# First norm of a decoder layer: scale and bias applied behind the transposes, with features on partitions

## The chip, the cores and the metric

The kernel runs on one core of a Trainium2 chip. The metric is the device time of one execution in microseconds (us). Five engines run their own instruction queues in order and meet through semaphores: TensorE (PE, matmuls; its weight loads are the rows PEld), VectorE (DVE), ScalarE (ACT), GpSimd (POOL) and SyncE (SP, which issues DMAs here). SBUF is the on-chip memory with 128 partitions, PSUM the memory that TensorE writes; one PSUM bank holds 128x512 floats.

## What is computed

A decoder layer over 512 tokens of 1024 features, all in float32. Only its beginning matters here:

```python
h = layer_norm(x, ln0_g, ln0_b)                  # (x - mu) * rsqrt(var + eps) * g + b
proj = h @ w_in[l]
q, f_logit, i_val, g_out, v_pool, gate_a, gate_b = jnp.split(proj, IN_SPLITS, axis=-1)
y_a = hgrn2_mixer(q, f_logit, i_val, g_out, ...) @ w_hg_branch[l]    # 8 recurrent heads
...
h = layer_norm(ALPHA * h + mix @ w_out[l], ln1_g[l], ln1_b[l])
...
```

So `h` has two readers: the projections, which want it with features on partitions, and the residual sum before the second norm, which wants it with tokens on partitions. What follows (mixers, expert retrieval over 16384 experts, a third norm) is the same in both programs.

## The kernel before

Tokens are worked on in four blocks of 128 (`NB`), features in eight chunks of 128 (`NCK`). The stage in question makes `h` and the first half of the values, `h @ w_in[:, 2048:2560]`:

- `load_x` and `load_w` issue DMAs on SP: each block of x as two halves of 256 KB, and four tiles of the value weights (`raw`, 512 KB each), two tiles to one buffer.
- `stats0` (VectorE, L277 and L279) takes mean and variance of a block, `deviation0` (ScalarE, L283) the square root, `affine0` (VectorE, L290, L293, L294) the norm: for each half of 512 features, (x - mean) * gain, and that times the reciprocal deviation plus bias. Gain and bias are the same for all tokens, so they are needed in every partition: four row loads of 2 KB (L299) and four matmuls of a row of ones with such a row (L312) put them into four PSUM banks `gb0`. The normalized block is `hres`, the residual.
- `transpose_split` turns a block by eight TensorE transposes (L162) into two PSUM banks `fp`, ScalarE copies each bank to the rounded part `xthi` (L167), VectorE subtracts to get the remainder `xtlo` (L168). A product of float32 matrices is three matmuls of such parts (`mm3`, L154 to L156).
- `split` makes the same two parts of a weight tile: a cast on ScalarE (`wh`, L149), a subtraction on GpSimd (`wl`, L150).
- `first_v(blk)` projects a block: 24 matmuls of 128x512 into a bank, which `put_v` copies out. Chunks 0 and 1 need the first weight tile, 2 and 3 the second, and so on.

The order of VectorE, ScalarE, SP and TensorE in this stage is that of the code (`manual_schedule`): for each block `affine0`, the next block's `stats0`, the transposes, the next block's `deviation0`, the weight tiles that `W0` names (the second and third behind block 0, the fourth behind block 1), and the projection of the block before. Eight matmuls on ones (`WARM`) stand ahead. GpSimd, and work that is coded outside that region, is placed by the scheduler that builds the program: small constants (`cmask`, `dtab`, `scT`, `pos` on GpSimd; `smask`, `reset`, `rc` on VectorE) are coded behind the stage and stand inside it in the queues.

Behind the stage `tok_half` does the second half of the values (L154 to L156 again), then the heads run: 36 tiles of the other projections in `slots`, with the attention parts `att0` to `att4` between them. `gain_bias(n)` loads gain and bias of a norm into all partitions, two DMAs of 512 KB.

## Time and profile before

| what | us |
|---|---|
| median of 3 runs | 1769.32 |
| lowest and highest run | 1764.86, 1771.26 |
| the profiled execution | 1768.82 |
| its span (first to last instruction) | 1767.1 |
| TensorE busy in the span | 1741.1 (99%) |
| VectorE busy in the span | 1317.2 (75%) |
| ScalarE, GpSimd busy | 799.1, 420.0 |

The profile is of one execution. The rows further down are read like this: start and length in us (a length with xN spans N instructions), engine, line of the kernel, operation, output <- inputs, shapes. What stands in brackets is the idle time of the engine just before and what ended it. A row's start plus its length is its end. The time of the profiled execution is 1.7 us more than its span.

### The profile page before, as it was taken

Reading aid. Unit: us, or ns where it says so; the run is one execution under the profiler, and the core shown is the slowest. Engines: PE = TensorE matmul, PEld = TensorE weight load, DVE = VectorE, ACT = ScalarE, POOL = GpSimd, SP = SyncE. Lnnn points to the kernel's source line nnn. Section 1 sums busy time; section 2 is a strip of 40 time slices with the busy share of each in tenths; the row PEclk is TensorE's granted clock in tenths of the full one; section 3 lists DMA queues with packets and bytes.
Section 4 is the critical chain, followed back from the end, with each engine's and each line's share of the span. In section 5 each row is a group of like instructions: output and inputs, shape, how many; then the busy total and the mean of one; then the engine's idle time right before and its main releaser. Section 6 shows DMA issues by size and latency. Waiting matters only on the chain.

```text
span 1767.1 us, 24739 instructions
## 1 busy us (share of the span) xinstructions
PE 1741.1 (99%) x9697; PEld 1536.8 (87%) x9697; DVE 1317.2 (75%) x2331; ACT 799.1 (45%) x1307; POOL 420.0 (24%) x293
## 2 busy tenths in 40 slices
PE   9999999999999999999999999999999999999997
PEld 6888887888788999998998888888888888888886
DVE  5467764154589889999847887878778787888777
ACT  3478862332332355665654444434444343344442
POOL 3533333443355540000011111112111111112110
PEclk9999999999999999999999999999999999999999
DMA  4322222332222325776787989889888889898872
GB/s 149 120 72 73 72 75 98 120 119 84 92 97 99 131 95 174 228 215 213 242 299 321 385 301 378 315 343 350 323 350 330 342 348 345 301 373 334 343 275 95
DMA packets 119789, 398.51 MB, mean 226 GB/s; under 512 B 8565, under 2 KB 71541, under 8 KB 83193
## 3 DMA queue, kind: packets, MB, share of 16 engines
q1 hardware_dynamic: 93752, 252.49, 39.2%
q0 software_dynamic: 18432, 134.23, 20.9%
q10 hardware_dynamic: 7488, 10.23, 1.6%
q8 instruction: 76, 1.25, 0.3%
q14 instruction: 41, 0.33, 0.1%
HBM read 359.42 MB, written 37.49 MB: 225 GB/s over the span
## 4 chain that ended last, share of the span: by engine, by line
PE 58%; issue 25%; DVE 10%; POOL 5%; ACT 1%; DMA 1%; POOLq 0%; ACTq 0%; DVEq 0%; SPq 0%
PE fp L154 11%; PE fp L156 11%; PE fp L155 11%; POOL rows L981 4%; PE yacc L155 4%; PE yacc L156 4%; PE yacc L154 4%; PE ple L858 3%; DVE A L893 2%; PE pG L907 2%; DVE oh L887 2%; DVE wl L232 2%; PE acc L155 1%; PE acc L156 1%; PE acc L154 1%
## 5 line engine op out<-in xcount | busy, mean ns | idle before, releaser
L154 PE MATMUL fp<-othi,wh 128*128 128x384 f32 (+1 forms) x1216 | 423.9, 349 | 1.1 <-ACT ge L646 0.8
L156 PE MATMUL fp<-othi,wl 128*128 128x384 f32 (+1 forms) x1216 | 418.8, 344 | 1.1 <-DVE wl L232 1.1
L155 PE MATMUL fp<-otlo,wh 128*128 128x384 f32 (+1 forms) x1216 | 418.0, 344 | 0.2 <-DVE otlo L168 0.2
L232 DVE TENSOR_TENSOR wl<-wraw,wh 128x1024 fp32r<-128x1024 f32 x246 | 300.9, 1225 | 153.7 <-ACT wh L231 153.1
L981 POOL DMA_INDIRECT rows<-in_uv_tab_dram,eidx x128 | 138.0, 1078 | 919.4 <-DVE hres L987 647.4
L231 ACT CAST wh<-wraw 128x1024 fp32r<-128x1024 f32 x280 | 293.4, 1049 | 19.5 <-DMA wraw<-in_wstream_dram 9.9
L155 PE MATMUL yacc<-wl,ah 128*128 128x512 f32 x768 | 300.3, 391 | 0.7 <-DVE wl L232 0.6
L156 PE MATMUL yacc<-wh,al 128*128 128x512 f32 x768 | 300.3, 391 | 0.0
L154 PE MATMUL yacc<-wh,ah 128*128 128x512 f32 x768 | 298.7, 389 | 0.0
L154 PEld LDWEIGHTS fp<-othi,wh 128*128 128x128 f32 x1216 | 228.7, 188 | 11.6 <-ACT ge L646 1.1
L155 PEld LDWEIGHTS fp<-otlo,wh 128*128 128x128 f32 x1216 | 228.8, 188 | 10.3 <-DVE otlo L168 0.5
L156 PEld LDWEIGHTS fp<-othi,wl 128*128 128x128 f32 x1216 | 228.4, 188 | 9.6 <-DVE wl L232 2.1
L150 POOL TENSOR_TENSOR wl<-wraw,wh 128x1024 fp32r<-128x1024 f32 x68 | 169.4, 2494 | 253.3 <-ACT wh L149 240.8
L997 ACT ACTIVATE hdot<-hdot 128x1 f32<-128x1 f32 x128 | 26.0, 203 | 344.6 <-DVE rows L996 344.6
L996 DVE SCALAR_TENSOR_TENSOR rows<-rows,hg 128x1024 f32<-128x1024 f32 x128 | 156.2, 1220 | 30.8 <-DMA rows<-in_uv_tab_dram,eidx 30.5
L155 PEld LDWEIGHTS yacc<-wl,ah 128*128 128x128 f32 x768 | 144.1, 188 | 30.5 <-DVE wl L232 1.9
L156 PEld LDWEIGHTS yacc<-wh,al 128*128 128x128 f32 x768 | 144.1, 188 | 30.3 <-DVE al L150 0.3
L646 ACT ACTIVATE ge<-fp 128x384 f32<-128x384 f32 x128 | 62.9, 491 | 234.7 <-PE fp L156 234.2
L154 PEld LDWEIGHTS yacc<-wh,ah 128*128 128x128 f32 x768 | 144.2, 188 | 28.4
L987 DVE SCALAR_TENSOR_TENSOR hres<-rows,hdot,hres 128x1024 f32<-128x1024 f32 x128 | 163.9, 1281 | 0.1
L154 PE MATMUL fp<-xthi,wh 128*128 128x512 f32 x352 | 142.5, 405 | 0.8 <-ACT sga L574 0.5
L156 PE MATMUL fp<-xthi,wl 128*128 128x512 f32 x352 | 137.3, 390 | 0.0
(246 smaller groups left out, 2494.2 us busy)
## 6 DMA issues: line engine op xcount, KB each, us to landing
wraw<-in_wstream_dram SPq DMA_DIRECT2D x140, 1024.0 KB
Gd<-stg SPq DMA_DIRECT2D x24, 1024.0 KB
gt<-Gd SPq DMA_DIRECT2D x16, 1536.0 KB
wraw<-in_w_in_dram SPq DMA_DIRECT2D x44, 512.0 KB
Hs<-ge ACTq DMA_DIRECT2D x52, 192.0 KB
ge<-Hs SPq DMA_DIRECT2D x52, 192.0 KB
wraw<-in_w_i_dram SPq DMA_DIRECT2D x8, 512.0 KB
wraw<-in_w_a_dram SPq DMA_DIRECT2D x8, 512.0 KB
```

What stands on the lines that cost most here:

```text
L150: lo_eng.tensor_sub(lo, src, hi.bitcast(FT))
L154: nc.tensor.matmul(o, a[0], b[0], start=start, stop=False)
L155: nc.tensor.matmul(o, a[0], b[1], start=False, stop=False)
L156: nc.tensor.matmul(o, a[1], b[0], start=False, stop=stop)
L231: nc.scalar.copy(hi, raw)
L232: (nc.gpsimd if i < split_at else nc.vector).tensor_sub(lo, raw, hi.bitcast(FT))
L646: nc.scalar.activation(ge, p[:, :ND], AF.Gelu)
L858: nc.tensor.matmul(o, a[x], b[y], start=(cc == 0 and blk % 2 == 0 and n == 0), stop=(cc == NCK - 1 and n == 2), skip_group_check=True)
L887: nc.vector.tensor_tensor(oh, iota2[:, None, :, :].to_broadcast([128, OG, 128, 2]), iT[:, t].rearrange("p a (u v) -> p (a u) v", v=2)[:, : ...
L981: nc.gpsimd.indirect_dma_start(out=got[n], out_offset=None, in_=ins["uv_tab"], in_offset=bass.IndirectOffsetOnAxis(ap=eidx[:, b, k:k + 1], ...
L987: nc.vector.scalar_tensor_tensor(hres[:, b, :], got.pop(n)[:, D:], hdot[:, b, k:k + 1], hres[:, b, :], op0=OP.mult, op1=OP.add)
L996: nc.vector.scalar_tensor_tensor(r, r, 1.0, hg[:, b, :], op0=OP.mult, op1=OP.mult, accum_out=hd)
```

## The change

Gain and bias now come as one small table `ln0_gb` with features on partitions (`lngb`, 128x16, one load at the head of SP's queue). `norm0` subtracts the mean and multiplies by the reciprocal deviation, without gain and bias. `rows0` transposes that, and scales and shifts the 128x128 transposed chunks in place in PSUM, where gain and bias are one number for each partition: the four chunks of the first bank on VectorE, the four of the second on ScalarE, each bank then copied and subtracted as before. `hres` holds the norm without gain and bias at first; `gain_bias(0)` loads both rows into all partitions, and eight VectorE operations of 128x1024, coded in the loop over `slots`, make the residual's rows. The broadcast matmuls, their row loads and their banks are gone; `WARM` goes from 8 to 13.

```diff
-WARM = 8
+WARM = 13
...
-        def affine0(blk):
+        def norm0(blk):
             mv = mv0[:, blk, :]
+            nc.vector.reciprocal(mv[:, 3:4], mv[:, 2:3])
             for half in range(2):
                 hs = slice(half * 512, (half + 1) * 512)
-                r = hres[:, blk, hs]
-                nc.vector.scalar_tensor_tensor(r, xq[blk // 2][:, blk % 2, hs], mv[:, 0:1], gb0["g"][half],
-                                               op0=OP.subtract, op1=OP.mult)
-                if half == 0:
-                    nc.vector.reciprocal(mv[:, 3:4], mv[:, 2:3])
-                nc.vector.scalar_tensor_tensor(r, r, mv[:, 3:4], gb0["b"][half], op0=OP.mult, op1=OP.add)
+                nc.vector.tensor_scalar(hres[:, blk, hs], xq[blk // 2][:, blk % 2, hs], mv[:, 0:1], mv[:, 3:4],
+                                        op0=OP.subtract, op1=OP.mult)
+
+        def rows0(blk):
+
+            ps = [psx.tile([128, 512], FT, name="fp", tag="fp") for _ in range(2)]
+            sl = slice(blk * 128, (blk + 1) * 128)
+            for c in range(NCK):
+                nc.tensor.transpose(ps[c // 4][:, c % 4 * 128:(c % 4 + 1) * 128], hres[:, blk, c * 128:(c + 1) * 128], ident)
+            for c in range(NCK):
+                p = ps[c // 4][:, c % 4 * 128:(c % 4 + 1) * 128]
+                g, b = lngb[:, 0, c:c + 1], lngb[:, 1, c:c + 1]
+                if c < 4:
+                    nc.vector.tensor_scalar(p, p, g, b, op0=OP.mult, op1=OP.add)
+                else:
+                    nc.scalar.activation(p, p, AF.Identity, scale=g, bias=b)
+                if c % 4 == 3:
+                    q = c // 4
+                    pv = ps[q].rearrange("p (c t) -> p c t", c=4)
+                    nc.scalar.copy(xthi[:, 4 * q:4 * q + 4, sl], pv)
+            if blk + 1 < NB:
+                stats0(blk + 1)
+            for q in range(2):
+                pv = ps[q].rearrange("p (c t) -> p c t", c=4)
+                hi = xthi[:, 4 * q:4 * q + 4, sl]
+                nc.vector.tensor_sub(xtlo[:, 4 * q:4 * q + 4, sl], pv, hi.bitcast(FT))
...
-            rows = [(w, half) for half in range(2) for w in "gb"]
-            for (w, half), t in zip(rows, gbrow):
-                nc.sync.dma_start(t[0:1, :], bass.AP(tensor=ins["ln0_" + w].tensor, offset=ins["ln0_" + w].offset + half * 512,
-                                                     ap=[[0, 1], [1, 512]]))
+            nc.sync.dma_start(lngb, ins["ln0_gb"])
...
             for _ in range(WARM):
-                nc.tensor.matmul(gb0["b"][1][:, 0:128], ones, ones, start=True, stop=True)
-            for (w, half), t in zip(rows, gbrow):
-                nc.tensor.matmul(gb0[w][half], ones[0:1, :], t[0:1, :], start=True, stop=True)
+                nc.tensor.matmul(warm[:, 0:128], ones, ones, start=True, stop=True)
...
             for blk in range(NB):
-                affine0(blk)
-                if blk + 1 < NB:
-                    stats0(blk + 1)
-                transpose_split(hres, xthi, xtlo, blk, psx)
+                norm0(blk)
+                rows0(blk)
...
+        g0, b0 = gain_bias(0)
         tok_half(ins["w_i"], 1, xthi, xtlo, put_v, nc.gpsimd, False)
...
             fn(arg)
+            if 3 <= n < 3 + NB:
+                r = hres[:, n - 3, :]
+                nc.vector.tensor_mul(r, r, g0)
+                nc.vector.tensor_add(r, r, b0)
```

Three places of the built queues show what moves. GpSimd, at the start of the program, before (`ident`, `cmask`, `dtab`, `scT`, `pos` are small constants, `wl` the low part of a weight tile):

```order
masks.py:199 AFFINE_SELECT ident<-ident 128x128
L369 MEMSET cmask 128x128
L379 MEMSET dtab_391 128x48
L379 MEMSET dtab_393 128x48
L384 MEMSET scT_395 128x512
L370 AFFINE_SELECT cmask<-cmask 128x128
L384 MEMSET scT_397 128x512
L532 IOTA pos 128x16
L150 TENSOR_TENSOR wl<-wraw,wh 128x1024 x68
```

and after:

```order
masks.py:199 AFFINE_SELECT ident<-ident 128x128
L150 TENSOR_TENSOR wl<-wraw,wh 128x1024
L383 MEMSET cmask 128x128
L393 MEMSET dtab_407 128x48
L393 MEMSET dtab_409 128x48
L398 MEMSET scT_411 128x512
L384 AFFINE_SELECT cmask<-cmask 128x128
L398 MEMSET scT_413 128x512
L547 IOTA pos 128x16
L150 TENSOR_TENSOR wl<-wraw,wh 128x1024 x67
```

The low part of the first weight tile, which waits for x's neighbour in the load queue and for ScalarE's cast, now stands ahead of the constants. On VectorE block 0 of the changed kernel reads those constants between its own steps (L289 is the norm, L302 the scaling of a transposed chunk, L276 and L278 the statistics of block 1, L314 the subtraction; `smask` is made of `cmask`, `rc` of `pos`):

```order
L289 TENSOR_SCALAR hres<-xq,mv_113 128x512
L113 CAST iota_81<-iota 128x256 [waits Pool_49]
L302 TENSOR_SCALAR fp<-fp,lngb 128x128 [waits DMAHW0_49,PE_49]
L302 TENSOR_SCALAR fp<-fp,lngb 128x128 [waits DVE_49] x2
L387 CAST smask<-cmask 128x128 [waits Pool_49]
L302 TENSOR_SCALAR fp<-fp,lngb 128x128 [waits DVE_49]
L276 BN_STATS st_112<-xq 128x6 [waits DMAHW4_49]
L276 BN_STATS st_112<-xq 128x6 [waits DMAHW5_49]
L553 TENSOR_SCALAR rc<-pos 128x16 [waits Pool_49]
```

Before, the same constants stood between the first and the second step of block 0's norm, behind fills that GpSimd had done by then. VectorE around block 3, before (L168 subtracts, L290 to L294 are the norm; block 2's subtractions stand first):

```order
L279 BN_AGGR mv_113<-st_112 128x2 [waits DVE_49]
L168 TENSOR_TENSOR xtlo<-fp,xthi 128x4x128 [waits Activation_49] x2
L290 SCALAR_TENSOR_TENSOR hres<-xq,mv_113,gb_118 128x512 [waits DVE_49]
L293 RECIPROCAL mv_113<-mv_113 128x1 [waits Activation_49]
L294 SCALAR_TENSOR_TENSOR hres<-hres,mv_113,gb_120 128x512 [waits DVE_49]
```

and after (L600 multiplies a block of the residual's rows by the gain, L601 adds the bias):

```order
L314 TENSOR_TENSOR xtlo<-fp,xthi 128x4x128 [waits Activation_49]
L600 TENSOR_TENSOR hres<-hres,gb 128x1024 [waits DMAHW5_49]
L314 TENSOR_TENSOR xtlo<-fp,xthi 128x4x128 [waits Activation_49]
L286 RECIPROCAL mv_113<-mv_113 128x1 [waits Activation_49]
L601 TENSOR_TENSOR hres<-hres,gb 128x1024 [waits DMAHW6_49,DVE_49]
L289 TENSOR_SCALAR hres<-xq,mv_113 128x512 [waits DVE_49]
L289 TENSOR_SCALAR hres<-xq,mv_113 128x512
L600 TENSOR_TENSOR hres<-hres,gb 128x1024
L302 TENSOR_SCALAR fp<-fp,lngb 128x128 [waits PE_49]
L601 TENSOR_TENSOR hres<-hres,gb 128x1024 [waits DVE_49]
```

The same alternation goes on through the scalings of block 3 until all eight row operations are done, the last of them between block 3's two subtractions. On SP the two loads of `gb` stand between the third and the fourth weight tile of the second half. Behind the stage both programs have the same rows on every engine in the same order, but for the eight row operations, which are not there any more.

## Rows read from the trace of the kernel before

**Rows 1.** Busy time by stretch: stretch, length, PE, PEld, DVE, ACT, POOL, clock, DMA, GB/s.

```profile
17.00:23.60 6.60, 4.48 (x22) 3.20 (x22) 6.46 (x12) 2.41 (x4) 5.91 (x3) 1.00 0.56 199
```

**Rows 2.** The chain that ended last, 18 to 24 us: start, length, what.

```profile
18.36 1.21 DVE st L277 x2
19.83 0.29 ACT mv L283
...
21.14 2.38 POOL wl L150
23.56 0.50 PE acc L155
```

**Rows 3.** Timeline, transposes of blocks 2 and 3, and projections behind them.

```profile
24.82 1.03 PE L162 MATMUL fp<-ident,hres 128*128 128x128 f32 x8
...
25.50 1.08 ACT L167 CAST xthi<-fp 128x512 fp32r<-128x512 f32 x2
...
31.15 1.03 PE L162 MATMUL fp<-ident,hres 128*128 128x128 f32 x8
...
31.94 0.47 PE L154 MATMUL acc<-wh,xthi 128*128 128x512 f32 x1
...
42.71 0.39 PE L156 MATMUL acc<-wh,xtlo 128*128 128x512 f32 x1
```

**Rows 4.** Timeline of the first 11 us: loads issued, constants, first weight tile.

```profile
0.81 0.34 SPq L299 DMA_DIRECT2D g<-in_ln_g_dram  x1
...
1.49 0.20 POOL L369 MEMSET cmask<- 128x128 f32 x1
...
2.05 0.83 SPq L271 DMA_DIRECT2D xq<-in_x_dram  x2
...
2.25 0.28 POOL L370 TENSOR_SCALAR_AFFINE_SELECT cmask<-cmask 128x128 f32<-128x128 f32 x1
...
7.24 1.04 ACT L149 CAST wh<-wraw 128x1024 fp32r<-128x1024 f32 x1 [0.27 <-DMA wraw<-in_w_i_dram]
...
8.37 2.35 POOL L150 TENSOR_TENSOR wl<-wraw,wh 128x1024 fp32r<-128x1024 f32 x1 [5.26 <-ACT wh L149]
```

**Rows 5.** Groups by line: line, engine, names, shapes, count | busy us, mean ns | idle.

```profile
L232 DVE TENSOR_TENSOR wl<-wraw,wh 128x1024 fp32r<-128x1024 f32 x246 | 300.9, 1225 | 153.7 <-ACT wh L231 153.1
...
L496 DVE SCALAR_TENSOR_TENSOR st<-st,all,pd 128x128 f32<-128x128 f32 x16 | 5.5, 341 | 0.3
...
L168 DVE TENSOR_TENSOR xtlo<-fp,xthi 128x512 fp32r<-128x512 f32 x8 | 5.0, 673 | 2.9 <-ACT xthi L167 2.9
...
L400 DVE TENSOR_SCALAR k<-f 128x512 f32<-128x512 f32 x8 | 3.4, 425 | 0.2
...
L513 ACT ACTIVATE o<-po 128x128 f32<-128x128 f32 x32 | 8.4, 279 | 1.2 <-PE po L508 1.2
...
L167 ACT CAST xthi<-fp 128x512 fp32r<-128x512 f32 x8 | 4.5, 593 | 7.0 <-PE fp L162 7.0
```

**Rows 6.** Timeline of VectorE and GpSimd among the heads, where they meet.

```profile
89.83 2.20 DVE L398 TENSOR_SCALAR f<-f,lbm 128x512 f32<-128x512 f32 x1 [2.77 <-ACT f L397]
...
124.40 0.68 DVE L441 TENSOR_TENSOR q<-q,bh 128x512 f32<-128x512 f32 x1
...
124.95 2.40 POOL L150 TENSOR_TENSOR wl<-wraw,wh 128x1024 fp32r<-128x1024 f32 x1 [3.24 <-ACT wh L149]
...
125.11 2.51 DVE L431 TENSOR_TENSOR half<-q,dtab 128x256 f32<-128x256 f32 x1
```

**Rows 7.** The row loads of the second norm: issue, and the slice of their end.

```profile
379.44 0.33 SPq L127 DMA_DIRECT2D gb<-in_ln_g_dram  x1
...
384.00:385.00 1.00, 1.00 (x6) 0.84 (x5) 0.80 (x2) 1.00 (x1) 0.00 (x0) 1.00 0.31 127
```

**Rows 8.** Timeline of TensorE, two projection matmuls of block 0.

```profile
15.88 0.63 PE L155 MATMUL acc<-wl,xthi 128*128 128x512 f32 x1
16.31 0.63 PE L156 MATMUL acc<-wh,xtlo 128*128 128x512 f32 x1
```

More of the change, by code (lines that the diff above doesn't have):

```diff
@@ L261, in hybrid_block @@
         mv0 = hp.tile([128, NB, 4], FT, name="mv0")
-        gbrow = [tmp("g0") for _ in range(4)]
-        gb0 = {w: [bank("gb0") for _ in range(2)] for w in "gb"}
+        lngb = smal.tile([128, 2, NCK], FT, name="lngb")
         wi = []
@@ L307, in hybrid_block @@
             load_x(3)
+            warm = bank("warm")
             for _ in range(WARM):
-                nc.tensor.matmul(gb0["b"][1][:, 0:128], ones, ones, start=True, stop=True)
-            for (w, half), t in zip(rows, gbrow):
-                nc.tensor.matmul(gb0[w][half], ones[0:1, :], t[0:1, :], start=True, stop=True)
+                nc.tensor.matmul(warm[:, 0:128], ones, ones, start=True, stop=True)
             stats0(0)
@@ L1151, in lay_out @@
         "ln0_g": a["ln0_g"], "ln0_b": a["ln0_b"],
+        "ln0_gb": c(np.stack([a["ln0_g"], a["ln0_b"]]).reshape(2, 8, 128).transpose(2, 0, 1)),
         "w_in": feat(w_in),
```

## The prediction

> **What bounds the kernel now.** I read the busy time by stretch first, then the chain of waits, then the timeline of the first 45 us, because everything that the change touches lies there: behind the first half of the value projection both programs have the same rows on every engine, in the same order. In the stretch that ends at 23.6 us TensorE is busy 4.48 of 6.60 us while VectorE is busy 6.46 [rows 1]: TensorE waits, VectorE feeds it. The chain says for what [rows 2]: statistics of token block 2 on VectorE (18.36), its square root on ScalarE (19.83), behind that the cast of the fourth weight tile, and GpSimd's low part of it, 21.14 to 23.51. TensorE goes on at 23.56. I call the end of that GpSimd row **S**. From S on TensorE never waits: block 2's transposes start at 24.82 (S + 1.31), block 3's at 31.15 (S + 7.64), block 2's projection at 31.94 (S + 8.43), and the last matmul of the half is at 42.71, so the next half starts at 42.93 (S + 19.42); 48 matmuls lie between 31.94 and 42.93, 0.23 us each [rows 3]. What comes after hangs on TensorE and on buffers that it frees, so a later start of that half moves the end of the kernel by as much. The question is thus where S falls, and whether TensorE still runs through from S.
>
> **Part 1: the start.** Removed: four row loads ahead of x on SP's queue, which held x's first issue until 2.05, and the four broadcast matmuls, for which VectorE's second step of block 0 waited. One load of the columns takes the place of the first. The first of the four went out at 0.81 and took 0.34; with x behind one load, at 1.2, x and the first weight tile come up to 0.84 us sooner, so the first cast starts near 6.4 instead of 7.24, and GpSimd's low part runs from about 7.5 to 9.85 [rows 4]. Normalizing costs two scalar operations of the form that takes 0.43 us [rows 5], so block 0 can be transposed about 7 us in; that is some 4 us ahead of now. The thirteen warm-up matmuls run beside the load and cost nothing.
>
> Then a queue takes it back. GpSimd's first low part now stands ahead of the small fills (the order shown with the change), and VectorE's mask cast stands between the third and fourth scaling of block 0. The fills up to the mask's select take 1.04 us, 1.49 to 2.53 [rows 4]; behind a low part that ends at 9.85 the mask is there at 10.9. So the fourth scaling ends not at 9.8 but at about **E = 11.6** (one cast and one scaling of at most 0.34 each, the row of a 128x128 operation that reads PSUM, [rows 5]). If the fill behind the select holds the cast up as well, some tenths more; without the mask 9.8. I take 11.6, since both queues are in order.
>
> **Part 2: one block's conversion.** Before, it was a copy and a subtraction. Now it is four scalings on VectorE, 0.34 to 0.37 each (1.4 us), the copy 0.59 [rows 5], four scalings on ScalarE at 0.28 to 0.32 (1.2), and a second copy: from the fourth VectorE scaling to the end of the second copy 2.4 us. No row shows the new forms; the bounds are the 0.28 and 0.34 of the nearest 128x128 rows and, above, the 0.43 of a scalar row four times as wide, which would add 1 us per block. I take the low end, to which the shape is nearest. So X, the end of block 0's second copy, is 14.0; square root and cast of the second weight tile follow, and GpSimd asks for its low part at X + 1.2 = 15.2 (now 15.81).
>
> **Part 3: who has the port.** In that same microsecond VectorE does the second subtraction of block 0 (the two reciprocals that stand ahead of it hold it to X + 0.3), the reciprocal, and the two normalizations of block 1, at X + 1.1 and X + 1.5. Rows show what happens then [rows 6]: GpSimd's subtraction at 124.95 began while VectorE's product at 124.40 still ran (0.68 us), and VectorE's next product, at 125.11, half as wide, took 2.51 us, until GpSimd was done. A scalar operation did the same at 89.83, 2.20 us against 0.43. The old steps read gain and bias from PSUM; the new ones have SBUF at both ends. So I expect the first normalization of block 1 to get in and the second to wait for GpSimd's 2.4 us: it ends at X + 4.2 = 18.2. The Trainium skill says it as a rule (SBUF — State Buffer, Who interferes with whom): a VectorE operation on both ports, or with two SBUF inputs, and a GpSimd operation exclude each other, and the second to start is blocked until the other is done. It speaks against this change, which turns PSUM operands into SBUF ones; by it the sum is the forecast, without it the rival of 1772, and the two rows agree with it (2.51 and 2.20 us, [rows 6]).
>
> Behind it: four scalings to 19.6, copies and scalings to 21.9, square root, cast and GpSimd's request at + 1.2, low part 2.4: S = 25.5, **2.0 us later** than 23.51. The same race at block 2 costs nothing, since its transposes come behind S anyway.
>
> **Part 4: the residual's rows.** In the code they stand beside the recurrent heads; in VectorE's queue they stand in this stage (second order shown with the change), between block 2's two subtractions and through the whole of block 3. They are eight operations of 128x1024 with two SBUF inputs, 1.22 us each by the subtraction of that size [rows 5], 9.8 us on VectorE; one that meets GpSimd would take up to 2.4 more [rows 6], but GpSimd has no tile to work on from S until projections free the weight buffers. From S: block 2's transposes at S + 1.3, their first bank ready 0.68 later [rows 3], scalings to S + 3.4, statistics 1.45, first subtraction to S + 5.5, **first row product to S + 6.7**, second subtraction to S + 7.4, reciprocal, **first row sum to S + 8.7**, normalization; block 3's transposes at S + 9.1 where TensorE is ready at S + 7.6: 1.5 us lost. From S + 9.45 VectorE does product, scaling, sum, scaling, product, scaling, sum, scaling (6.2 us: S + 15.65), ScalarE copies to S + 16.3, VectorE does the last product and the subtraction, S + 17.45. Block 3's projection could start at S + 15.35; its third matmul needs that subtraction, and 22 matmuls of 0.23 follow from S + 17.5: S + 22.5 against S + 19.42. **3.1 us lost** in all; were the rows elsewhere, nothing, and this term is bounded by 0 and by the 9.8 us of the rows.
>
> Gain and bias of the rows are two loads of 512 KB on SP, behind a weight load that waits for S. At 379.44 such a pair was issued behind two weight loads of the same size, and the four were through in the slice that ends at 385.0, within some 5 us of the pair's issue [rows 7]. Here one weight load is ahead: gain at about S + 4.4, bias at S + 5.9, and VectorE asks at S + 5.5 and S + 7.5. Hidden, with about 1 us to spare.
>
> **Sum.** + 2.0 (S) + 3.1 (from S on) = + 5.1 us. The profiled execution took 1768.82 us, its span 1767.1; that is 0.5 under the median of the runs shown, 1769.32. 1768.8 + 5.1 = **1774**. 0.5%, about what a measurement of this kernel can tell from no change, is 8.8 us: the forecast is a loss that lies within it.
>
> **The rivals.**
> - *No half is blocked* (VectorE's second normalization gets in first): the low part starts near X + 1.9 and block 1 goes on at once, S about 23.8, + 0.3 + 3.1: **1772**. For it: the race is decided by 0.3 us, and scalings on ScalarE of 0.38 or more would turn it.
> - *Both halves are blocked* (GpSimd asks before X + 1.1; the first normalization waits for one low part, the second for the next): 2.4 us more, **1776**. For it: the first gets in by 0.1 us only.
> - *TensorE falls to its low clock.* It would stand nearly idle for some 3.5 us before S. The granted clock reads 1.00 [rows 1], yet in this stage matmuls of one shape start 0.43 us apart at 15.88 and 16.31 [rows 8] against 0.23 later, as at 1.2 and 2.4 GHz. Block 1's 24 matmuls at the low level cost 4.9 us more, of which block 3's wait hides 1.5: **1778**, half of it beyond 0.5%. Against it: the present wait of 1.3 us [rows 2] changes nothing.
> - *The row loads land late*: the one that makes the kernel slower by over 0.5%. Place: the first row product. Price: each us by which gain lands after S + 5.5 goes to block 3 in full. It decides from S + 9.2, 3.7 us behind that point, which makes + 8.8: about 8.7 us from issue to landing, against some 5 in [rows 7]. **1782**.
> - *The early start survives*: the mask and the scalings cost less, S comes at 20 to 21, and half of the rows' loss stays: **1767**. That the rows run beside the heads, as the change says, would give that too; the built queue speaks against it.
>
> **How the numbers follow.** Forecast 0.42, none blocked 0.15, both blocked 0.20, low clock 0.10, late loads 0.05, early start 0.08. Range: from the early start, 1767, to the low clock and the upper end of "both blocked", 1780; beyond are the late loads and the tails. Slower by over 0.5%: late loads 0.05, half of the low clock 0.05, the top of "both blocked" 0.04: 0.14. Faster by over 0.5% would need S at 12 us: 0.02. Within: 0.84.
>
> **What would show it.** Right: the mask cast of block 0 starting behind GpSimd's fills, near 11; one normalization of block 1 with over 2 us; GpSimd's fourth low part ending at 25 to 26; eight 1.2 us rows on VectorE around block 3, with TensorE idle before block 3's transposes and before its third projection matmul; the second half starting near 48. Wrong: a fourth low part before 22, row products that stand at 70 us or later, or a later stage that is longer or shorter by itself.

## The result and the profile after

The changed kernel takes **1779.85 us** (median of 7 runs, 1776.45 to 1782.66); the kernel before, run beside it, 1766.93 (7 runs, 1764.86 to 1771.81). The ratio is 1.0072, with a 95% interval from 1.0059 to 1.0085: slower, by a little more than the 0.5% that can be told from no change. The profiled execution took 1779.85, its span 1778.0 against 1767.1: 10.9 us more. The forecast was 1774, the range 1767 to 1780.

The 10.9 us fall into three parts, read at three places in the trace: S (the end of the fourth low part on GpSimd, 23.51 before), the end of the first half of the value projection (the copy of block 3's sum, L267 before and L266 after), and the end of the kernel.

| place | before | after | shift | of which new here |
|---|---|---|---|---|
| S | 23.51 | 27.50 | +4.0 | 4.0 |
| copy of block 3, first half | 43.13 | 50.55 | +7.4 | 3.4 |
| span | 1767.1 | 1778.0 | +10.9 | 3.5 |

Nearly all of the last 3.5 us is there by 459 us, where the shift is +10.7. Behind that point the same rows take from 3.2 us less to 3.3 us more than in the profile of before, in the profiles of the runs below, so a difference of that size in one span tells nothing of the change.

Up to S. The chain of waits of after between 7 and 28 us (start, length, what), which answers to [rows 2]:

```profile
7.22 1.06 ACT wh L149
8.35 2.34 POOL wl L150
...
11.44 0.25 POOL cmask L384
...
18.93 2.54 POOL wl L150
...
25.12 2.39 POOL wl L150
27.56 0.51 PE acc L155
```

and the timeline of VectorE, ScalarE and GpSimd for it (start, length, engine, line, operation, names, shapes, count, idle time ahead and who ended it):

```profile
8.21 1.33 DVE L302 TENSOR_SCALAR fp<-fp,lngb 128x128 f32<-128x128 f32 x3 [0.16 <-PE fp L297]
11.72 0.51 DVE L387 CAST smask<-cmask 128x128 uint8<-128x128 f32 x1 [2.19 <-POOL cmask L384]
11.87 0.56 DVE L302 TENSOR_SCALAR fp<-fp,lngb 128x128 f32<-128x128 f32 x1
...
14.80 0.59 ACT L308 CAST xthi<-fp 128x512 fp32r<-128x512 f32 x1
...
16.22 3.04 DVE L289 TENSOR_SCALAR hres<-xq,mv 128x512 f32<-128x512 f32 x2
...
16.60 4.88 POOL L150 TENSOR_TENSOR wl<-wraw,wh 128x1024 fp32r<-128x1024 f32 x2 [4.31 <-ACT wh L149]
...
25.12 2.38 POOL L150 TENSOR_TENSOR wl<-wraw,wh 128x1024 fp32r<-128x1024 f32 x1 [3.65 <-ACT wh L149]
```

Three scalings of block 0 are through by 9.54; then VectorE waits 2.19 us for the mask, the fourth scaling ends at 12.43, the second copy at 15.39 (X). The two normalizations of block 1 take 3.04 us, and they run into GpSimd's two low parts, which begin at 16.60. The groups by line show what the new operations cost (busy us, mean ns of one), where [rows 5] had 341 and 279 ns for the nearest ones:

```profile
L304 ACT ACTIVATE fp<-fp,lngb 128x128 f32<-128x128 f32 x16 | 6.9, 433 | 0.4
L302 DVE TENSOR_SCALAR fp<-fp,lngb 128x128 f32<-128x128 f32 x16 | 6.8, 427 | 2.6 <-PE fp L297 2.3
...
L600 DVE TENSOR_TENSOR hres<-hres,gb 128x1024 f32<-128x1024 f32 x4 | 4.9, 1220 | 0.0
```

From S on. TensorE's timeline (the transposes of blocks 2 and 3, the third projection matmul of block 3), and the windows before and behind S (stretch, length, busy time and count of PE, PEld, DVE, ACT, POOL, granted clock, DMA share, GB/s), which answer to [rows 3] and [rows 1]:

```profile
28.83 1.89 PE L297 MATMUL fp<-ident,hres 128*128 128x128 f32 x8
...
37.11 1.18 PE L297 MATMUL fp<-ident,hres 128*128 128x128 f32 x8
...
45.12 0.50 PE L156 MATMUL acc<-wh,xtlo 128*128 128x512 f32 x1 [0.37 <-DVE xtlo L314]
```

```profile
11.80:25.40 13.60, 10.41 (x26) 7.21 (x27) 11.64 (x26) 8.80 (x17) 5.64 (x5) 0.50 0.49 171
28.90:32.20 3.30, 3.30 (x13) 2.94 (x12) 2.19 (x6) 1.06 (x2) 0.00 (x0) 0.50 0.93 290
```

The clock granted in these two stretches is the lower level, 1.2 GHz. In the kernel before it reads 1.00 from 17.00 to S [rows 1]; but ahead of that, at 15.88 and 16.31, its matmuls, too, start 0.43 us apart [rows 8]. Block 2's transposes at 28.83 take 1.89 us instead of 1.03.

Behind the first half nothing is queued differently, and yet 3.5 us are added. The four sums of the second half are copied one behind the other, each when its last three matmuls are done, so the length of that row tells how far apart matmuls start. Of before and of after:

```profile
62.85 2.63 ACT L267 COPY vtok<-acc 128x512 f32<-128x512 f32 x4 [2.30 <-PE acc L156]
```

```profile
70.85 2.69 ACT L266 COPY vtok<-acc 128x512 f32<-128x512 f32 x4 [2.40 <-PE acc L156]
```

One copy takes 0.59, and from the start of the first to that of the last are 9 matmuls: 2.63 - 0.59 = 2.04 us, 0.2267 each, against 2.10, 0.2333. No engine waits; the matmuls themselves come 6.7 ns later. The experiments start there.

### The profile page after: what moved, and what is told of

Its sections match the earlier page's. It is cut to its first block, busy times and chain, and to the rows that moved or that the text cites. A ratio compares the mean times of both kernels' runs of the same rounds, so it can differ in the third digit from the quotient of the medians.

```text
span 1778.0 us, 24770 instructions
## 1 busy us (share of the span) xinstructions
PE 1744.1 (98%) x9699; PEld 1538.7 (87%) x9699; DVE 1329.9 (75%) x2347; ACT 806.1 (45%) x1323; POOL 420.8 (24%) x293
## 3 DMA queue, kind: packets, MB, share of 16 engines
q8 instruction: 76, 1.25, 0.3%
## 4 chain that ended last, share of the span: by engine, by line
PE 57%; issue 25%; DVE 10%; POOL 5%; DMA 2%; ACT 1%; POOLq 0%; SPq 0%; ACTq 0%; DVEq 0%
PE fp L154 11%; PE fp L156 11%; PE fp L155 11%; POOL rows L1000 5%; PE yacc L155 4%; PE yacc L156 4%; PE yacc L154 4%; PE ple L877 3%; DVE A L912 2%; PE pG L926 2%; DVE oh L906 2%; DVE wl L232 2%; PE acc L156 1%; PE acc L155 1%; PE acc L154 1%
```

## The experiments

All compare with the kernel before, run on the same chip in the same sitting. S and the end of the first half are from each one's profile.

| run | kernel | median us | ratio to before (95%) | S | copy of block 3 |
|---|---|---|---|---|---|
| - | changed kernel | 1779.85 | 1.0072 (1.0059 to 1.0085) | 27.50 | 50.55 |
| e1 | xthi 128 bytes behind its place | 1782.06 | 1.0090 (1.0074 to 1.0105) | 28.26 | 52.28 |
| e2 | kernel before, xthi moved 64 bytes | 1771.03 | 1.0020 (1.0012 to 1.0029) | 23.53 | 43.60 |
| e3 | rows pinned beside the heads | 1788.26 | 1.0128 (1.0107 to 1.0149) | 28.33 | 49.99 |
| e4 | fills early | 1778.16 | 1.0063 (1.0045 to 1.0081) | 27.47 | 50.67 |
| e5 | xthi at its exact place | 1775.49 | 1.0052 (1.0039 to 1.0064) | 28.28 | 52.28 |
| e6 | all fills early | 1776.94 | 1.0066 (1.0051 to 1.0082) | 27.15 | 50.44 |
| e7 | half of the norm on ScalarE | 1777.96 | 1.0069 (1.0056 to 1.0082) | 27.41 | 52.27 |
| e8 | kernel before, all tiles moved | 1765.57 | 0.9994 (0.9985 to 1.0003) | 23.51 | 43.15 |
| e9 | e5, small casts at the stage's end | 1774.38 | 1.0057 (1.0044 to 1.0070) | 24.82 | 48.81 |
| e10 | e9, next block's norm ahead | 1769.27 | 1.0024 (1.0015 to 1.0033) | 22.73 | 44.80 |
| e11 | e10, rows behind the first half | 1768.57 | 1.0013 (1.0001 to 1.0025) | 23.65 | 45.76 |
| e12 | e11, TensorE kept busy ahead of S | 1765.94 | 1.0000 (0.9991 to 1.0009) | 21.67 | 42.40 |

### Behind the first half: where xthi lies (e1, e2, e5, e8)

What differs between the two programs for a matmul of the second half is the place of its operands. The change puts a tile of 64 bytes per partition (`lngb`) ahead of `xthi` and `xtlo`; these begin at byte 192,160 of each partition before and at 192,224 after, while the weight tiles (the first at 84,128) have not moved. The distance between the two was a multiple of 256 bytes before and is 64 more now. The first try took another 64:

```
-        lngb = smal.tile([128, 2, NCK], FT, name="lngb")
+        lngb = smal.tile([128, 4, NCK], FT, name="lngb")[:, 0:2, :]
```

> The changed kernel with 64 bytes per partition added to the tile of gain and bias columns, so that xthi and xtlo stand 128 bytes behind their place of before instead of 64; nothing else differs. Behind the first half of the value projection the changed kernel loses about 3.5 us more, and its matmuls that read xthi start 0.233 us apart at 36 to 75 us instead of 0.227. Theory A (the place of the operand in SBUF sets the pace): 0.227 apart again, and 3.5 to 4 us less than the changed kernel, about 1776. Rival B (the pace comes from the order of the banks or from chance in the phases): still 0.233, time within 1 us of the changed kernel, 1780.

It did not get better: 1782.06, a ratio whose interval overlaps that of the changed kernel. With 128 bytes the matmuls stay slow, 0.2322 in the second half (2.68 - 0.59 over 9), and through the head tiles more is lost than in the changed kernel (table below):

```profile
72.49 2.68 ACT L266 COPY vtok<-acc 128x512 f32<-128x512 f32 x4 [2.39 <-PE acc L156]
```

So the guess that 128 bytes are as good as none was wrong, and this run alone spoke for the rival. The run beside it decided. It moves `xthi` and `xtlo` in the kernel before, by 64 more bytes per partition in a small tile that stands ahead of them:

```
-            lbraw = smal.tile([128, 2, NCK], FT, name="lbraw")
+            lbraw = smal.tile([128, 4, NCK], FT, name="lbraw")[:, 0:2, :]
```

> The kernel before with 64 bytes per partition added to a small tile that stands ahead of xthi, so that xthi and xtlo stand where the changed kernel has them; nothing else differs. Theory A: matmuls of the second half of the value projection start 0.233 us apart instead of 0.227, those of the head tiles 0.229 instead of 0.227, and the kernel takes 3.5 to 4 us more, about 1770.5. Rival B: 0.227 throughout, 1767.

```profile
63.90 2.69 ACT L267 COPY vtok<-acc 128x512 f32<-128x512 f32 x4 [2.41 <-PE acc L156]
```

No instruction changes its place in its queue, S stays at 23.53, and the loss is there: 1771.03, 0.20% over before, 3.3 us. The two runs that follow close it from the other side: the changed kernel with `xthi` exactly where it was,

```
-        lngb = smal.tile([128, 2, NCK], FT, name="lngb")
+        lngb = hp.tile([128, 2, NCK], FT, name="lngb")
```

> The changed kernel with the tile of gain and bias columns taken from the pool behind xthi and xtlo, so that these two stand exactly where the kernel before has them; every instruction and its order are the changed kernel's. The run before this showed that 128 bytes further is not the same place as before (0.2325 us), so what counts is not the distance modulo 128. Theory A (place): matmuls of the second half 0.2267 apart, the loss behind the first half gone, 3.5 us under the changed kernel, 1776. Rival B (something else in the changed order makes them slower): 0.233, 1780.

and the kernel before with every tile moved together:

```
-    eps = consts.tile([128, 2], FT, name="eps")
+    eps = consts.tile([128, 26], FT, name="eps")
```

> The kernel before with 96 bytes added to its first small tile, so that every tile of the kernel moves by 96 bytes together: xthi, the weight tiles and the other TensorE operands keep their distances and start at multiples of 256. Theory A1 (what counts is how stationary and moving operand stand to each other): spacing 0.2267 and the time of before, 1767. Theory A2 (what counts is the start of each operand by itself): the spacing of all stages changes, since all operands start elsewhere: by 0.006 of 0.227 either way on 5,000 matmuls, some 15 to 30 us; less if starting at a multiple of 256 is best, more if not.

Of the first and of the second:

```profile
72.05 2.63 ACT L266 COPY vtok<-acc 128x512 f32<-128x512 f32 x4 [2.30 <-PE acc L156]
```

```profile
62.87 2.63 ACT L267 COPY vtok<-acc 128x512 f32<-128x512 f32 x4 [2.30 <-PE acc L156]
```

Both are at 0.2267 again. e8 takes the time of before, e5 1775.49: 1.0052 against 1.0072 for the changed kernel, which is the 3.5 us expected, though the two intervals overlap a little. (Its profiled execution is the slowest of its five, 1780.88; the excess arises behind 459 us.) How far each is behind the kernel before, at four places of the trace (the copies of block 3 and of the second half, the first sigmoid of the gates, the first copy of the per-layer projection):

| run | 43.13 | 62.85 | 318.79 | 449.40 |
|---|---|---|---|---|
| changed kernel | +7.42 | +8.00 | +9.49 | +10.70 |
| e1 (128 bytes) | +9.15 | +9.64 | +13.76 | +14.96 |
| e2 (before, 64 bytes) | +0.47 | +1.05 | +2.74 | +3.68 |
| e5 (exact place) | +9.15 | +9.20 | +9.21 | +8.66 |
| e8 (before, all moved) | +0.02 | +0.02 | +0.30 | -0.27 |

The loss grows only where `xthi` or `xtlo` is an operand and lies at another distance from the other operand. Among the head tiles, matmuls that read them start 0.2276 us apart in the kernel before, 0.2293 in the changed kernel, 0.2326 in e1 and 0.2277 in e5. Between the gates and the output projection stand matmuls that read `othi`, which only e8 moves, and it moves the weights along with it: in all five kernels of the table and in the kernel before these start 0.2267 apart. With 64 bytes the loss is 3.3 us behind the first half in the changed kernel and 3.2 in e2, where another 0.5 arose within that half. That the place costs it is shown. That it is the distance between the two operands and not the start of each is what e8 says, which starts each of them elsewhere; by which part of the chip, and which distances count as the same, is not shown: only a multiple of 256 bytes and 64 and 128 more were tried. The Trainium skill (SBUF — State Buffer, Who interferes with whom) lists two read ports of TensorE, one for the moving operand and one for the weight load, as independent. The runs would differ from that if these two are what meets here, which no run shows: 2.04 us or 2.10 us for the same nine matmuls by the place of one operand.

e5 also shows how much the first stage varies: its first weight tile landed 0.8 us later than in the profile of after, and the whole 0.8 is in S (28.28 against 27.50). From the start of the first low part to S it takes 19.15 us in the profile of after, and 19.14 to 19.16 in e1, e3 and e5. That is new as well. In e8 the first low part began 2.09 us later than in the kernel before (10.46 against 8.37, [rows 4]) and S did not move. The changed kernel has hung the fills, and through the mask the first block, behind that tile.

### Up to S: three waits behind one another (e4, e6, e9)

The mask cast waits because GpSimd makes the mask behind its first low part. e4 writes the code of mask, decay tables and score tiles ahead of the stage:

> The changed kernel with the code of mask, decay tables and score tiles ahead of the first stage, so that GpSimd makes them before its first low part and the mask cast of block 0 does not wait. Theory: the fourth scaling of block 0 ends near 10.2 instead of 12.4, everything up to S comes 2.0 to 2.3 us sooner (S near 25.3) and the kernel with it: about 1777.7. Rival 1: the wait turns into another (GpSimd's low part, a weight tile that lands late), S stays within 0.5 us of 27.5: 1779.5. Rival 2: with block 0 sooner the second normalization of block 1 gets in before GpSimd: S near 23, 1775.5.

S stayed (27.47), and the ratio is within the interval of the changed kernel's. But in this profile the first weight tile came later: its low part began at 9.42, not at 8.35, and from there to S it is 18.05 us instead of 19.15. So 1.1 us of the 2.0 to 2.3 expected were gained, and a late tile hid them. The rest did not come, because the mask was there and the next small operation took its place in the wait, a row of counts that reads the iota `pos`:

```profile
11.89 0.17 DVE L554 TENSOR_SCALAR rc<-pos 128x16 f32<-128x16 f32 x1 [2.78 <-POOL pos L548]
```

With the iota early too (e6):

> The changed kernel with mask, decay tables, score tiles and, this time, the small position row made ahead of the first stage. Without the position row moved, the wait for the mask (2.19 us) came back as a wait for that row (2.78 us). Theory: the fourth scaling of block 0 ends near 9.8 instead of 12.4; GpSimd asks for the second low part 2.4 us sooner, and S is 25.0 to 25.3 instead of 27.5, the kernel near 1777.5. Rival 1: block 0 waits for its first low part or weight tile instead, S above 26.5, 1779. Rival 2: the second normalization of block 1 comes before GpSimd's request and is not blocked: S near 23, 1775.5.

No operand was missing any more, and S still came at 27.15 (18.28 us behind the start of the first low part, 0.9 less than in the changed kernel; 2.2 to 2.5 were expected):

```profile
8.87 2.34 POOL L150 TENSOR_TENSOR wl<-wraw,wh 128x1024 fp32r<-128x1024 f32 x1 [5.77 <-ACT wh L149]
...
8.92 2.39 DVE L554 TENSOR_SCALAR rc<-pos 128x16 f32<-128x16 f32 x2
```

Two operations of 128x16, which take 0.17 us at other times, hold VectorE from 8.92 to 11.31: GpSimd's low part runs from 8.87 to 11.21. It is the wait for GpSimd again, the prediction's port, met by the smallest operation in the queue. e9 (from e5) makes the fills early and writes the casts and counts at the end of the first stage:

```
             lb, omlb = lbm[:, 4, :], lbm[:, 5, :]
+            smask = smal.tile([128, 128], U8, name="smask")
+            nc.vector.tensor_copy(smask, cmask)
+            rcs = [counts(2), counts(4)]
```

> The kernel of the exact place (1775.5 us), with the mask cast and the two small count rows written at the end of the first stage in VectorE's queue and GpSimd's fills ahead of it. With the fills early, the position row, and then the count rows, each still met GpSimd's first low part in VectorE's queue (2.2, 2.8 and 2.4 us); here none of them stands there. Theory: the fourth scaling of block 0 ends near 9.6, the second copy at 12.6; the second normalization of block 1 is still blocked; S near 24.5, kernel near 1772.5. Rival: the second low part or block 1 waits for something else (a weight tile, the first low part that ends at 10.7 to 11.5), S at 26.5 or later, 1775.

```profile
7.99 1.78 DVE L302 TENSOR_SCALAR fp<-fp,lngb 128x128 f32<-128x128 f32 x4 [0.15 <-PE fp L297]
...
13.56 3.04 DVE L289 TENSOR_SCALAR hres<-xq,mv 128x512 f32<-128x512 f32 x2
...
13.93 4.89 POOL L150 TENSOR_TENSOR wl<-wraw,wh 128x1024 fp32r<-128x1024 f32 x2 [2.75 <-ACT wh L149]
```

The fourth scaling ends at 9.77, as the prediction had it for a block without the mask (9.8), and S is 24.82 (24.5 expected). In the total no gain is shown: the median, 1774.38, is 1.1 us under that of e5 where 3 were expected, but the ratio to the kernel before is no better (1.0057 against 1.0052). The five runs lie between 1771.37 and 1777.82, and the profiled one, 1771.37, is the lowest of them. In S the step is 2.7 us against the changed kernel.

### The port (e7, e10)

By the port the prediction means the access to SBUF for which an operation of VectorE waits until GpSimd's is done, or the other way round. e7 gives the second half of each block's normalization to ScalarE:

> The changed kernel with the second half of each block's normalization on ScalarE (scale 1/deviation, bias minus mean over deviation, one small VectorE operation more) instead of VectorE; fills and rows as in the changed kernel. Theory (port): no VectorE operation of the first stage is held by GpSimd's low part; the ScalarE half stands behind two weight casts and ends near 18.2 where the blocked one ended at 19.26, so S is near 26.4 and the kernel 1 us under the changed one. Rival: GpSimd's low part is not what holds the second normalization (it is slow by itself): its ScalarE form ends no sooner than 19.2, and the first one stays at 0.5 us but nothing is gained: 1780.

Up to S no VectorE normalization is held any more (0.54 us for the one half that is left), and from X to S it takes 11.16 us instead of 12.11, the 1 us expected. Nothing of it is kept. ScalarE's half of block 2 stands behind the copy of block 0's sum, and that waits for TensorE:

```profile
28.93 0.59 ACT L266 COPY vtok<-acc 128x512 f32<-128x512 f32 x1 [4.10 <-PE acc L156]
29.42 0.81 ACT L291 ACTIVATE hres<-xq,mv 128x512 f32<-128x512 f32 x1
```

The first half ends at S + 24.86 where the changed kernel has S + 23.05, and the ratio is that of the changed kernel.

e10 leaves the operations as they are and moves them: statistics, root and normalization of the next block come between the two low-part subtractions of a block, ahead of GpSimd's request.

```
+                if c == 3 and blk + 1 < NB:
+                    stats0(blk + 1)
+                if c == 6 and blk + 1 < NB:
+                    deviation0(blk + 1)
...
                 nc.vector.tensor_sub(xtlo[:, 4 * q:4 * q + 4, sl], pv, hi.bitcast(FT))
+                if q == 0 and blk + 1 < NB:
+                    norm0(blk + 1)
```

> As the run ahead of it, and the next block's statistics, square root and normalization stand between the two low-part subtractions of a block, with the square root between ScalarE's third and fourth scaling, so that block 1 is normalized before GpSimd's second low part starts. Theory (port): both normalizations of block 1 take 0.5 us each, the fourth low part ends some 2.3 us sooner against the end of block 0's second copy: S 22.2 to 22.8, kernel near 1770.5. Rival: ScalarE, which now has copies, scalings and casts in a row, sets S: 24 or later, 1772.5.

```profile
11.86 1.00 DVE L289 TENSOR_SCALAR hres<-xq,mv 128x512 f32<-128x512 f32 x2
...
13.59 4.70 POOL L150 TENSOR_TENSOR wl<-wraw,wh 128x1024 fp32r<-128x1024 f32 x2 [2.60 <-ACT wh L149]
...
20.38 2.35 POOL L150 TENSOR_TENSOR wl<-wraw,wh 128x1024 fp32r<-128x1024 f32 x1 [2.09 <-ACT wh L149]
```

The same two operations take 1.00 us, and S is 22.73, 2.1 us sooner than in e9 and 0.8 sooner than before the change. That the second normalization is held by GpSimd, and by nothing in itself, is shown.

### The residual's rows and the clock (e3, e11, e12)

e3 puts the rows where the change says they are, by pinning each product behind the VectorE work of its slot:

```
-                nc.vector.tensor_mul(r, r, g0)
+                tc.keep_in_program_order(nc.vector.tensor_mul(r, r, g0))
```

> The changed kernel with each row product pinned behind the VectorE work of its slot, so that the residual's rows stand beside the recurrent heads in VectorE's queue too; xthi stays where the changed kernel has it. Theory: block 3's transposes and its third projection matmul no longer wait, the second half starts about 3.3 us earlier (S + 19.6 instead of S + 22.75), and all of it is kept: about 1776.5. Rival: VectorE is what the heads wait for there, so that eight operations of 1.22 us cost as much beside them: 1779 to 1780, with the second half starting 3 us earlier and the gain gone by 320 us.

1788.26, the slowest of all, and beyond what either the theory or the rival had. In the first stage the rows' going gave 1.4 us (from S to the copy of block 3: 21.66 instead of 23.05), not 3.3. With the rows gone TensorE runs block 2's transposes and its next matmuls at the low level, 29.8 to 33.2,

```profile
29.80:33.20 3.40, 3.40 (x14) 3.01 (x12) 2.50 (x6) 1.37 (x3) 0.00 (x0) 0.50 0.91 294
```

and block 3's transposes come at S + 9.39, hardly sooner than the S + 9.61 of the changed kernel. Two reasons held the same place, and each hides the other. In the changed kernel itself TensorE hardly waits for the normalization there: it is done with the matmuls ahead only at 37.07, because of the low level from 28.90 to 32.20. With the rows in the same place and the clock at 1.00 it does wait, 1.48 us in e10, where the transposes come at S + 9.28. Of the changed kernel and of e10:

```profile
33.20:37.30 4.10, 4.06 (x19) 2.97 (x18) 4.10 (x7) 1.77 (x5) 0.00 (x0) 1.00 0.44 175
```

```profile
32.01 0.66 PE L297 MATMUL fp<-ident,hres 128*128 128x128 f32 x4 [1.48 <-DVE hres L289]
```

Among the heads the rows then cost 11.6 us (the shift against before is 7.90 at 103 us and 19.47 at 146.5). The waits of TensorE there, from 100 to 150 us, of which the changed kernel has none (engine, line, waited for: us, times, longest):

```profile
PE po L523 <- DVE st L511: 7.3, 4, 4.3
```

and, for the first of these waits, why VectorE is late with the state `st`:

```profile
105.84 2.62 POOL L150 TENSOR_TENSOR wl<-wraw,wh 128x1024 fp32r<-128x1024 f32 x1 [6.24 <-ACT wh L149]
...
106.10 3.44 DVE L600 TENSOR_TENSOR hres<-hres,gb 128x1024 f32<-128x1024 f32 x1
```

A row product meets a low part and takes 3.44 instead of 1.22, and the attention's state, for which TensorE waits, stands behind it; around the waits the granted clock is 0.89 (105 to 120 and 135 to 150 us). The longest wait, 4.3 us, stands behind an operation of the heads that met a low part (L456, 2.82 us from 138.77), behind two row operations; that the rows brought that meeting about is not shown by itself. The queue that had been built, with the rows in the first stage, was the better one. e11 puts them directly behind block 3's last subtraction, beside the second half:

> As the run ahead of it, and the residual's rows stand in VectorE's queue directly behind the last subtraction of block 3, ahead of the head constants, so that they run beside the second half of the value projection. Theory: what the rows cost in block 3 goes (1.4 to 2 us) and nothing comes back, since VectorE has little to do up to 65 us: 1768.5 to 1769, within the uncertainty of the kernel before. Rival: eight operations with SBUF at both ends block GpSimd's low parts of the second half, TensorE waits for those: at or above the run ahead of it.

The gain is within the measurement (1768.57 against 1769.27): the rows are out of the way, but the clock fell ahead of S, where in e10 it had stayed at 1.00 (S is also 0.9 us later, with the first low part 1.0 us later):

```profile
20.00:25.00 5.00, 1.79 (x4) 1.29 (x5) 1.17 (x3) 1.22 (x2) 2.35 (x1) 0.71 0.09 19
25.00:30.00 5.00, 5.00 (x19) 4.16 (x19) 2.80 (x6) 1.65 (x4) 0.00 (x0) 0.61 0.90 317
```

TensorE was busy 1.79 of these 5 us; from 22.1 to 28.9 the clock was at the low level. e12 fills the wait:

```
+                    keep(12)
                     first_v(0, range(CS))
...
+                    first_v(0, range(CS, NCK - 2))
+                    keep(14)
+                    first_v(0, range(NCK - 2, NCK))
```

> As the run ahead of it, with 12 idle matmuls of 128 columns behind block 0's transposes and 14 ahead of the fourth weight tile's products of block 0; they write a bank that nothing reads, in time in which TensorE waits. In the run ahead of it the granted clock is 0.50 from 22.1 to 28.9, and from S to the second half it takes 22.1 us against 19.6 in the kernel before. Theory (clock): with TensorE kept busy in the wait ahead of S the clock stays at 1.00 behind S, the second half starts at S + 19.7 to 20.3, and the kernel takes 1.8 to 2.5 us less, 1766 to 1766.8, level with the kernel before. Rival: the clock falls all the same, or the idle matmuls run at the low clock and stand in the way: 1768.5 or more.

```profile
20.00:25.00 5.00, 5.00 (x41) 4.69 (x40) 0.31 (x1) 0.59 (x1) 1.68 (x1) 1.00 0.45 155
25.00:30.00 5.00, 5.00 (x24) 4.10 (x24) 4.68 (x12) 2.90 (x7) 0.00 (x0) 1.00 0.76 281
```

The clock is 1.00 throughout, S is 21.67 (block 1's transposes, too, ran at the full clock), the copy of block 3 comes at 42.40, and the kernel takes 1765.94, a ratio of 1.0000: level with the kernel before, and clear of e10's 1.0024. Against e11's 1.0013 the intervals overlap, so in the total this step by itself is not shown. In the stage it is: from S to the copy of block 3 it takes 22.07 us in e10 (rows there, clock at 1.00), 22.11 in e11 (rows gone, low level), 20.73 in e12 (rows gone, clock at 1.00) and 19.62 in the kernel before. The idle matmuls ran to 22.8, 1.2 us beyond S at 21.67, so there are a few too many of them; fewer were not tried.

## Why the prediction was right or wrong

**What bounds the kernel: right.** TensorE goes on at S in every variant of the changed kernel (in e12 0.9 us behind it, because of the idle matmuls), and S is set by the chain of scalings, copies, root, cast and low part that the prediction followed.

**Part 1, the start: the wait was right, its start was not.** The mask cast stands behind GpSimd's fills at 11.72 (10.9 forecast). "x and the first weight tile come up to 0.84 us sooner" held for x, whose load went out at 1.25 instead of 2.05 and whose first statistics began at 3.99 instead of 4.81, but not for the weight tile: the first cast began at 7.22 as before (7.24, [rows 4]), and the fills hang on it. E, the end of the fourth scaling, was 12.43, not 11.6. That two more operations stood ready behind the mask to wait in its place was not seen; taking out one gave S about 1 us, and only with all out did block 0 stop waiting (e4, e6, e9).

**Part 2, one block's conversion: mis-sized.** The low end, 0.28 to 0.34, was taken; it is the upper bound that came true, 427 and 433 ns. From E to X it takes 2.96 us, not 2.4, and X was 15.39, not 14.0. The row of the same kind, 0.43 at four times the width, was nearer than the rows of the same size.

**Part 3, the port: right in kind and size.** The first normalization of block 1 got in, the second waited, 3.04 us for the two; the rivals "none blocked" and "both blocked" did not come. From X to S it is 12.11 against 11.5. S went up by 4.0 instead of 2.0: 0.8 from the start, 0.6 from block 0's scalings and copies, 0.6 from X to S, where ScalarE's scalings of block 1 took longer than forecast.

**Part 4, the rows: the sum was right, its cause only in part, and there by luck.** All eight stand at 1.22 us in the first stage; block 3's transposes came at S + 9.61 (9.1 forecast), the third projection matmul at S + 17.62 (17.5), the second half at S + 22.75 (22.5). The 1.5 us that TensorE was to wait ahead of block 3's transposes were there in e10 (1.48); in the changed kernel the low clock stood in that place and cost as much. And "were the rows elsewhere, nothing" is wrong twice: without them 1.4 us of the 3.4 go (e3), because the low clock holds the same place, and beside the heads they cost 11.6. The row loads were hidden, as forecast.

**The rival of the low clock came with the forecast, not instead of it.** The prediction counted its price against the rows' wait ("of which block 3's wait hides 1.5"), and so it was: the last matmul ahead of block 3's transposes starts at S + 9.17, in the kernel before at S + 7.41, and these 1.8 us stand where the rows' wait would have been. Its price was too high, 4.9 us for 24 matmuls; the low level lasted 3.3 us behind S. (1774 + 4.9 - 1.5 is 1777.4, not 1778, and block 0's transposes at 7 are 5 us ahead of 11.96, not 4; neither changes the forecast.)

**What failed outright is the step "a later start of that half moves the end of the kernel by as much".** Another 3.5 us arose behind it, from the place of two tiles that the change moves by 64 bytes (e2, e5). The sum was 5.8 us too low, 2.3 us in the first stage (7.4 against 5.1) and 3.5 behind it; the result stands 0.15 us inside the upper end of the range, and that is luck: the range had been drawn for other causes, the low clock and two blocked halves, and the kernel before, from which the forecast counts, ran 2 us faster beside the changed one (1766.93) than in the profile (1768.8). The prediction named "a later stage that is longer or shorter by itself" as what would show it wrong; but no row of the profile of before shows what a tile's place costs. "Slower by over 0.5%" had been given 0.14, for causes of which only the low clock came, and in part.

## What to carry to other kernels

A VectorE operation that reads and writes SBUF can cost the whole of what GpSimd is doing at that moment, whether it is 128x1024 or 128x16; so look at every instruction in VectorE's queue that a low part of GpSimd can meet, not only at the ones that the change speaks of. A wait that is taken away in an in-order queue shows the next one behind it, so count on a gain only when the whole row of them has been read. When a small tile is added, compare the addresses of the matmul operands before and after, or put it behind them: here the trace shows a difference only as matmuls that start a few ns further apart.

## What the runs showed of the hardware

- Matmuls of 128x512 started 0.2267 or 0.2333 us apart by where `xthi` lies against the other operand: 64 bytes cost 3.3 us (e2), 128 bytes more up to 449 us in one profile (e1: the shift grows by 5.8 us from 43 to 449 us, in the changed kernel by 3.3), and moving all tiles by 96 bytes nothing (e8: 0.9994).
- Two operations of 128x16 on VectorE, 0.17 us at other times, took 2.39 us beside a low part of GpSimd (e6). The Trainium skill's rule (SBUF — State Buffer, Who interferes with whom) that the one that comes second is blocked until the other is done agrees with it.
- A scaling of 128x128 in PSUM with one number per partition takes 427 ns on VectorE and 433 ns on ScalarE.
- TensorE's granted clock fell to 0.50 behind stretches in which it mostly waited (after: 11.8 to 25.4 and 28.9 to 32.2; e11: 22.1 to 28.9), and matmuls that do nothing, put into the wait, kept it at 1.00 (e12): from S to the copy of block 3 20.73 us against 22.11 (e11).
